# Twelve gate channel tiles done singly instead of ten, and operand roundings and sigmoids queued behind the weights in the output stage

## The chip, the cores and the metric

The kernel runs on one core of one Trainium2 chip. The metric is the device time of one execution in microseconds. The core's engines are TensorE (PE, with its weight loads shown apart as PEld), VectorE (DVE), ScalarE (ACT), GpSimd (POOL) and SyncE (SP). In this kernel SP and POOL issue the transfers. Every engine works through its own list of instructions in order and waits at an instruction until what it needs is there.

## The reference

One layer of a bidirectional encoder for two sequences, a prompt (b = 0) and a sample (b = 1), each 1024 rows by 1024 channels in float32. Cut to what matters here:

```
xn = rmsnorm(x, g_pre)
fv, fg, hv, hg, mg = split(xn @ w_in)
y_f = (real(fft2(fv)) * silu(fg)) @ w_fourier_out
v, x1, x2 = split(short_conv(hv, w_short))
z = v
for n, gate in enumerate((x1, x2)):
    z = gate * long_conv(z, filter_n)
y_h = (z * silu(hg)) @ w_hyena_out
g_f, g_h = split(sigmoid(mg + b_merge))
out = (g_f * y_f + g_h * y_h) @ w_out
y = x + rmsnorm(out, g_post)
```

The gates of a sequence are four sections of `xn @ w_in`, called by number in the kernel: 0 is `fg`, 4 is `hg`, 5 and 6 are the two halves of `mg`. Each has 1024 channels, which is 8 channel tiles of 128.

## The kernel before

**Numbers in two parts.** Float32 products are made on PE from operands split into a rounded part h and a remainder l: `split` (line 168) rounds with a copy on ACT and subtracts on DVE or POOL. A product is three matmuls, h·h, h·l and l·h (`mm3`, line 369; `times`, line 954). So before a weight or an operand can be used, it is loaded, rounded on ACT (tile `wh`, `sf`, `sh`) and subtracted (tile `wl` and the second part of `sf`, `sh`).

**Who sets the order.** The program is written as a sequence, and a scheduler gives each engine its list: it takes what its own model holds to be ready, and of that what stands earlier in the program. `with tc.issue_after(x)` puts everything in the block that runs on the engine of x behind x in that engine's list. It is an order of issue and no wait for the end of x, and it says nothing to other engines.

**The stages.** After the Fourier branch and the filters come, in this order:

1. The long convolutions (`branches`, line 897): for each sequence a list of 16 steps (sequence, order, channel tile). Step i traces the front of step i+1, then `conv_back` of step i (line 789; forward matmuls into `pX`, products with the filter on DVE, back matmuls into `pT`). For the second sequence the last steps also do gate channel tiles singly with `spill_gate` (line 757): `inproj` (line 714) multiplies all 8 blocks of the sequence by two weight halves into two PSUM tiles `pin`, ACT copies them out, SP stores them. Which tiles are done singly stands in `PLAIN` (line 969). Its tiles are taken from the end of the list: with four, three and two steps left, two each. The four that remain follow behind the last matmul of the last convolution (line 949).
2. The gates of the second sequence that are not in `PLAIN` (`phase_gates`, line 971): a pair of channel tiles (c, c+1) by two column halves is one job, done with seven products in place of eight, from sums of weights and sums of the sequence's blocks (`prepare` and `sums`). With the ten tiles in `PLAIN` there are 11 jobs. The tiles in PSUM are called `pg`.
3. The output stage (`phase_out`, line 1079): four units (sequence, half of the rows). A unit makes 8 projections by `w_fo` from the operands `sf` (tile `pyf`), then 8 by `w_ho` from the operands `sh` (`pyh`). `project` (line 1114) takes two weight halves, each loaded by POOL's queue in `weight` (line 1101), with three buffers in turn; each half is 12 matmuls. `operand` (line 1091) loads one of the 8 operand tiles of the next group and splits it at once, one in each projection. `gated` (line 1123) loads a gate tile by SP's queue, takes its sigmoid on ACT with a bias and multiplies the projection by it on DVE; gate tiles have three buffers. `beside` (line 1136) loads, rounds and sums blocks of `w_out` for the next stage, on ACT behind the sigmoid of its projection. In the last unit `sum4` loads and splits parts of a sum of `w_out` blocks (`t4`).
4. The last rows (`last_rows`), the product with `w_out` by seven products, tiles `po`.

Of the kernel before, what the change touches and what calls it, by code (L numbers as in the profile page):

```python
# [9 lines left out]
F32 = mybir.dt.float32  # L10
F32R = mybir.dt.float32r
I32 = mybir.dt.int32
AF = mybir.ActivationFunctionType
# [148 lines left out]
class K:  # L162
# [626 lines left out]
    def conv_back(self, n, ct, B, ws):  # L789
# [3 lines left out]
        for g, pairs in GROUPS:  # L793
# [34 lines left out]
            def tt(name):  # L828
                return ws.tile([P, 512], F32, tag="tt", name=name, bufs=4)
# [3 lines left out]
            elif g == 3:  # L833
                S_, D_ = tt("S"), T[1]
                self.add("dve", S_, T[1], Tp)
# [61 lines left out]
    def branches(self, nb, nct, ws):  # L897

        tc, nc = self.tc, self.nc
        steps = []
        for b in range(nb):
            steps.append((b, 0, 0))
            for c in range(1, nct):
                steps += [(b, 0, c), (b, 1, c - 1)]
            steps.append((b, 1, nct - 1))
        plain = list(self.PLAIN)
        Z, X = {}, {}

        def front(i):
            b, n, c = steps[i]
            src = self.conv(1, c, ws, "v", b) if n == 0 else Z.pop(c)
            return self.conv_front(src, ws)

        def gates(i):
            b, n, c = steps[i]
            x = self.conv(2 + n, c, ws, f"x{n + 1}", b)
            if n and b == 0:
                early = c < NH  # L920
                ps = None if early else self.inproj(4, c)
                for q in range(2):
                    sg = self.wp.tile([P, 512], F32, tag="gt", name="sg", bufs=3)
                    if early:
                        nc.sync.dma_start(sg, self.d_g[0][4][c][:, 512 * q:512 * q + 512])
                    nc.scalar.activation(sg, sg if early else ps[q], AF.Silu)
                    self.mul("pool", x[:, 512 * q:512 * q + 512], x[:, 512 * q:512 * q + 512], sg)
            X[i] = x
        B = front(0)
        gates(0)  # L930
        for i, (b, n, c) in enumerate(steps):
            nxt = None
            if i + 1 < len(steps):
                nxt = front(i + 1)
                gates(i + 1)
                if i + 2 < len(steps) and steps[i + 2][0] != steps[i + 1][0]:
                    self.load_x(steps[i + 2][0])
            y = self.conv_back(n, c, B, ws)
            B = nxt
            for _ in range({4: 2, 3: 2, 2: 2}.get(len(steps) - i, 0)):  # L940
                self.spill_gate(b, *plain.pop(), ws)
            z = self.gate(n, c, y, X.pop(i))
            if n == 0:
                Z[c] = z
                continue
            nc.sync.dma_start(self.d_sh[b][c], z)
            if b == 0 and NF <= c:
                self.spill_gate(0, 0, c, ws)
        with tc.issue_after(self.ended.ins):
            for sec, c in plain:  # L950
                self.spill_gate(1, sec, c, ws)
# [14 lines left out]
        self.stt("dve", s[:, 1], s[:, 0], -1.0, r[:, 3], MUL, SUB)  # L966
        self.add("dve", s[:, 3], s[:, 1], r[:, 2])

    PLAIN = [(5, 0), (5, 1), (6, 0), (6, 1), (5, 2), (5, 3), (6, 2), (6, 3), (5, 4), (5, 5)]

    def phase_gates(self):

# [3 lines left out]
        wp, b = self.wp, 1  # L976
        jobs = [(s, c) for c in range(0, 8, 2) for s in (0, 4, 5, 6) if (s, c) not in self.PLAIN]
        with ExitStack() as es:
# [100 lines left out]
    def phase_out(self):  # L1079
# [3 lines left out]
        tc, nc, a = self.tc, self.nc, self.a  # L1083
        wp, xp = self.wp, self.xp
        units = [(b, half) for b in range(NB) for half in range(2)]
        with ExitStack() as es:
# [4 lines left out]
            def operand(i, nm, k):  # L1091

                b, half = units[i]
                src = (self.d_g[b][0] if nm == "f" else self.d_g[b][4] if b else self.d_sh[b])[k][:, 512 * half:512 * half + 512]
                t = xp.tile([P, 2, 512], F32R, tag=f"x{'hl'[k // 4]}{k % 4 + 4 * (nm == 'h')}", name=f"s{nm}{k}", bufs=1)
                r = t[:, 1].bitcast(F32)
                nc.sync.dma_start(r, src)
                self.split(t[:, 0], t[:, 1], r, "dve", "act")
                return t[:, 0], t[:, 1]

            def weight(w, dt, q):


                own = self.nw % 3 == 2
                self.nw += 1
                pool, nb = (op, 1) if own else (wp, 2)
                r = pool.tile([P, 512], F32, tag="w", name="wr", bufs=nb)
                nc.gpsimd.dma_start(r, a[w][dt][:, 512 * q:512 * q + 512])
                h = pool.tile([P, 4, P], F32R, tag="wh", name="wh", bufs=nb)
                l = pool.tile([P, 4, P], F32R, tag="wl", name="wl", bufs=nb)  # L1110
                self.split(h.rearrange("p a b -> p (a b)"), l.rearrange("p a b -> p (a b)"), r, "dve", "act")
                return h, l

            def project(i, nm, w, dt, S):
                ps = self.psum("mm", 4, f"py{nm}")
                for q in range(2):
                    h, l = weight(w, dt, q)
                    for kk in range(4):
                        k = 4 * q + kk
                        self.mm3(ps, (h[:, kk], l[:, kk]), S[k], k == 0, k == 7)  # L1120
                return ps

            def gated(i, dt, ps, sec, bias, out):
                b, half = units[i]
                g = wp.tile([P, 512], F32, tag="gt", name="g", bufs=3)
                self.fetched = nc.sync.dma_start(g, self.d_g[b][sec][dt][:, 512 * half:512 * half + 512])
                self.opened = nc.scalar.activation(g, g, AF.Sigmoid, bias=self.bm[:, bias:bias + 1])
                out = g if out is None else out
                self.mul("dve", out, ps, g)
                return out  # L1130
# [51 lines left out]
            def sum4(k):  # L1182
                h, l = [sp.tile([P, 512], F32R, tag=f"yf{2 * k + j}", name=f"t4{'hl'[j]}{k}", bufs=1) for j in range(2)]
                r = l.bitcast(F32)
                nc.sync.dma_start(r, self.d_t[1][:, k])
                self.split(h, l, r, "dve", "act")
                T4.append((h, l))

            with tc.issue_after(self.copied.ins):
                S = {(0, "f"): [operand(0, "f", k) for k in range(8)]}  # L1190
            gp = oc.tile([P, D], F32, name="gp")
            nc.sync.dma_start(gp, a["g_post"][0].partition_broadcast(P))
            for i, (b, half) in enumerate(units):
                Yf = []
                S[i, "h"] = []
                for dt in range(8):
                    ps = project(i, "f", "w_fo", dt, S[i, "f"])
                    S[i, "h"].append(operand(i, "h", dt))
                    y = sp.tile([P, 512], F32, tag=f"yf{dt}", name=f"yf{dt}", bufs=1)
                    Yf.append(gated(i, dt, ps, 5, dt, y))  # L1200
                    beside(i, dt)
                S[i + 1, "f"] = []
                for dt in range(8):
                    ps = project(i, "h", "w_ho", dt, S[i, "h"])
                    if i + 1 < len(units):
                        S[i + 1, "f"].append(operand(i + 1, "f", dt))
                    g = gated(i, dt, ps, 6, 8 + dt, None)
                    self.add("dve", Yf[dt], Yf[dt], g)
                    nc.sync.dma_start(self.d_m[i][:, :, dt], Yf[dt].rearrange("p (t c) -> p t c", t=4))
                    beside(i, 8 + dt)  # L1210
                    if i == 3 and dt % 2 == 1:
                        sum4(dt // 2)
            block = lambda j: [(BH[k][:, j], BL[k][:, j]) for k in range(4)]
            T = [[(TH[k][:, j], TL[k][:, j]) for k in range(4)] for j in range(2)]
            self.last_rows(units, block(0), block(1), block(2), T1, T[0], T[1], T4, gp, op)
# [196 lines left out]
```

## Time and profile before

| | |
|---|---|
| median of 3 runs | 2494.66 us (2486.66 to 2496.76) |
| the profiled execution | 2485.07 us, span 2483.2 us, granted TensorE clock 0.997 |
| PE busy | 2407.4 us, 97% of the span, 13184 matmuls |
| PE weight load busy | 2081.4 us, 84% |
| DVE busy | 1955.9 us, 79% |
| ACT busy | 1102.2 us, 44% |
| POOL busy | 498.6 us, 20% |
| moved by DMA | 429.39 MB, mean 173 GB/s |

The span runs from the first to the last instruction of the profiled execution; 1.9 us of its time lie around it. A matmul is shown with a modelled length that reaches over the start of the next one, so the time that one really takes is the distance from its start to the next start. In rows of instructions in order of time the first number is the start in us from the start of the span, the second the length; "x4" joins four instructions that follow each other, and the bracket gives the idle time of the engine ahead of the row and what ended it. In rows of waits, "A <- B: 70.2, 49, 5.5" says that the instruction A waited for B for 70.2 us in 49 cases, 5.5 us at most.

### The profile page before, as it was taken

The page shows a single profiled execution, that of the slowest core. Times are in us where ns is not written, and L with a number is a line of the kernel's source. Part 1 is how long each engine was busy: PE and PEld are TensorE (multiplying, and loading weights), DVE is VectorE, ACT ScalarE, POOL GpSimd, SP SyncE. Part 2 cuts the span into 40 slices and gives each one's busy share as a digit, 9 for nine tenths or more (in the row PEclk, how much of TensorE's full clock was granted, in tenths as well). Part 3 has the DMA queues.
Part 4 walks back from the last instruction along what each step waited for, and adds up shares of the span by engine and source line. Part 5 has one row for each costly group of instructions (what it writes and reads, how often), then busy time and mean ns, then how long its engine had stood idle before and what let it go on. Part 6 is the DMA issues. An engine that isn't in the chain of part 4 may idle for free.

```text
span 2483.2 us, 37239 instructions
## 1 busy us (share of the span) xinstructions
PE 2407.4 (97%) x13184; PEld 2081.4 (84%) x13184; DVE 1955.9 (79%) x3737; ACT 1102.2 (44%) x2043; POOL 498.6 (20%) x514
## 2 busy tenths in 40 slices
PE   6999999999989999999999999999999999999998
PEld 6988888888878888888888888887888787878786
DVE  7786788888798999999889999876655456655677
ACT  5546666666653333333222233333443445444443
POOL 1331222212233333441000000212000111212121
PEclk9999999999999999999999999999999999999999
DMA  7536545444555554545343443435443567675543
GB/s 272 191 113 225 196 157 162 162 163 158 177 184 184 180 174 167 171 154 193 123 149 137 137 141 123 140 132 182 168 163 136 196 219 252 237 245 201 161 166 127
DMA packets 224867, 429.39 MB, mean 173 GB/s; under 512 B 23510, under 2 KB 87223, under 8 KB 224168
## 3 DMA queue, kind: packets, MB, share of 16 engines
q1 hardware_dynamic: 197868, 332.29, 40.1%
q0 software_dynamic: 26624, 94.70, 10.9%
q8 instruction: 104, 1.70, 0.3%
q14 instruction: 83, 0.68, 0.1%
q10 hardware_dynamic: 188, 0.02, 0.0%
HBM read 290.60 MB, written 136.31 MB: 172 GB/s over the span
## 4 chain that ended last, share of the span: by engine, by line
PE 44%; DMA 5%; DVE 3%; issue 1%; ACT 1%; SPq 0%; DVEq 0%; POOL 0%; ACTq 0%
PE pin L194 14%; PE pg L194 8%; PE po L194 6%; PE pyf L194 5%; PE pT L194 4%; PE pyh L194 4%; PE pX L194 3%; DMA oraw<-in_w_out 1%; PE tph L785 1%; DMA xraw<-d_x 1%; DMA mraw<-d_m 1%; DMA sh<-d_g 1%; DMA wr<-in_w_fo 1%; DMA wh<-d_w 0%; DMA d_m<-yf 0%
## 5 line engine op out<-in xcount | busy, mean ns | idle before, releaser
L194 PE MATMUL pin<-xh,wh 128*128 128x512 f32 x1440 | 563.8, 392 | 4.4 <-DVE v L177 1.8
L194 PE MATMUL pin<-xh,wl 128*128 128x512 f32 x1440 | 563.0, 392 | 1.6 <-POOL wl L181 1.6
L194 PE MATMUL pin<-xl,wh 128*128 128x512 f32 x1440 | 564.2, 392 | 0.0
L181 POOL TENSOR_TENSOR wl<-wr,wh 128x512 fp32r<-128x512 f32 x132 | 250.0, 1895 | 1132.2 <-ACT wh L171 1093.5
L194 PEld LDWEIGHTS pin<-xh,wh 128*128 128x128 f32 x1440 | 271.1, 188 | 54.6 <-DVE v L177 2.0
L194 PEld LDWEIGHTS pin<-xh,wl 128*128 128x128 f32 x1440 | 271.3, 188 | 51.6 <-POOL wl L181 2.5
L194 PEld LDWEIGHTS pin<-xl,wh 128*128 128x128 f32 x1440 | 271.3, 188 | 49.5
L171 ACT CAST wh<-wr 128x512 fp32r<-128x512 f32 x260 | 159.8, 618 | 227.2 <-PE pin L194 102.6
L194 PE MATMUL pT<-cinv,yh 128*128 128x256 f32 x1024 | 193.2, 283 | 0.5 <-ACT yh L171 0.5
L194 PEld LDWEIGHTS pT<-cinv,yh 128*128 128x128 f32 x1024 | 165.5, 191 | 10.1 <-ACT yh L171 0.9
L181 DVE TENSOR_TENSOR t<-pX,k 128x1024 f32<-128x1024 f32 x128 | 155.6, 1216 | 11.0 <-PE pX L194 7.6
L194 PE MATMUL pyh<-sh,wh 128*128 128x512 f32 x512 | 157.9, 391 | 3.5 <-ACT wh L171 3.5
L194 PE MATMUL pX<-bh,cfwd 128*128 128x256 f32 x768 | 160.4, 287 | 0.6 <-DVE t L181 0.6
L194 PE MATMUL pyf<-sf,wh 128*128 128x512 f32 x512 | 157.6, 391 | 1.6 <-ACT wh L171 1.6
L194 PE MATMUL pT<-cinv,yl 128*128 128x256 f32 x512 | 145.8, 285 | 5.1 <-DVE yl L181 5.0
L171 ACT CAST yh<-y 128x512 fp32r<-128x512 f32 x128 | 79.7, 622 | 158.6 <-DVE y L181 125.5
L171 ACT CAST bh<-b 128x512 fp32r<-128x512 f32 x144 | 88.9, 621 | 119.5 <-DVE b L181 81.2
L181 DVE TENSOR_TENSOR wl<-wr,wh 128x512 fp32r<-128x512 f32 x128 | 87.2, 686 | 67.1 <-ACT wh L171 67.0
L194 PEld LDWEIGHTS pX<-bh,cfwd 128*128 128x128 f32 x768 | 125.5, 190 | 4.0 <-DVE t L181 1.0
L181 DVE TENSOR_TENSOR bl<-b,bh 128x512 fp32r<-128x512 f32 x144 | 110.3, 767 | 21.9 <-ACT bh L171 21.8
L194 PEld LDWEIGHTS pyh<-sh,wh 128*128 128x128 f32 x512 | 95.5, 188 | 25.4 <-ACT wh L171 6.2
L194 PEld LDWEIGHTS pyf<-sf,wh 128*128 128x128 f32 x512 | 95.6, 188 | 23.1 <-ACT wh L171 3.7
(348 smaller groups left out, 5385.6 us busy)
## 6 DMA issues: line engine op xcount, KB each, us to landing
k<-d_k SPq DMA_DIRECT2D x128, 512.0 KB, 4.0
wr<-in_w_in SPq DMA_DIRECT2D x132, 256.0 KB, 3.1
d_g<-gt SPq DMA_DIRECT2D x124, 256.0 KB, 2.3
d_k<-kt SPq DMA_DIRECT2D x128, 128.0 KB, 2.2
d_k<-kt SPq DMA_DIRECT2D x64, 256.0 KB, 2.3
wr<-in_w_fo POOLq DMA_DIRECT2D x64, 256.0 KB, 3.6
g<-d_g SPq DMA_DIRECT2D x64, 256.0 KB, 3.9
wr<-in_w_ho POOLq DMA_DIRECT2D x64, 256.0 KB, 3.5
```

Of the source, the lines that this page charges most:

```text
L171: self.rounded = nc.scalar.copy(h, src)
L181: e.tensor_tensor(out, a, b, op=op)
L194: return self.nc.tensor.matmul(out, lhsT, rhs, start=start, stop=stop, skip_group_check=shared)
L785: nc.tensor.transpose(tp[:, q * P:(q + 1) * P], eo[:, e, q], self.ident)
```

## The change

There are two parts. In the first, tiles (6, 4) and (6, 5) join `PLAIN`, so they are done singly, their job leaves the seven-product stage (10 jobs stay), and the last step takes two tiles as the three before it do. The pairs move by one step, since they are taken from the end of the list.

In the second, the loading and the splitting of an operand in the output stage are two functions. `weight` keeps the instruction with which ACT rounds the latest weight half (`self.weighed`). The new function `ahead` splits the operand that the projection before has loaded, on ACT behind that rounding, and loads the next one; after the last projection of a group it is called once more for the last split. The sigmoid of a gate, too, is queued on ACT behind the rounding of the second weight half of its projection. The first eight operands of the first unit are split at once as before.

```diff
@@ branches
-            for _ in range({4: 2, 3: 2, 2: 2}.get(len(steps) - i, 0)):
+            for _ in range({4: 2, 3: 2, 2: 2, 1: 2}.get(len(steps) - i, 0)):
                 self.spill_gate(b, *plain.pop(), ws)
-    PLAIN = [(5, 0), (5, 1), (6, 0), (6, 1), (5, 2), (5, 3), (6, 2), (6, 3), (5, 4), (5, 5)]
+    PLAIN = [(5, 0), (5, 1), (6, 0), (6, 1), (5, 2), (5, 3), (6, 2), (6, 3), (5, 4), (5, 5), (6, 4), (6, 5)]
@@ phase_out
-                r = t[:, 1].bitcast(F32)
-                nc.sync.dma_start(r, src)
-                self.split(t[:, 0], t[:, 1], r, "dve", "act")
+                nc.sync.dma_start(t[:, 1].bitcast(F32), src)
+                return t
+
+            def rounded(t):
+                self.split(t[:, 0], t[:, 1], t[:, 1].bitcast(F32), "dve", "act")
                 return t[:, 0], t[:, 1]
...
                 self.split(h.rearrange("p a b -> p (a b)"), l.rearrange("p a b -> p (a b)"), r, "dve", "act")
+                self.weighed = self.rounded
                 return h, l
...
+            def ahead(i, nm, dt):
+
+                S_ = S.setdefault((i, nm), [])
+                with tc.issue_after(self.weighed.ins):
+                    if dt:
+                        S_[-1] = rounded(S_[-1])
+                if dt < 8:
+                    S_.append(operand(i, nm, dt))
+
             def gated(i, dt, ps, sec, bias, out):
...
-                self.opened = nc.scalar.activation(g, g, AF.Sigmoid, bias=self.bm[:, bias:bias + 1])
+                with tc.issue_after(self.weighed.ins):
+                    self.opened = nc.scalar.activation(g, g, AF.Sigmoid, bias=self.bm[:, bias:bias + 1])
...
-                S = {(0, "f"): [operand(0, "f", k) for k in range(8)]}
+                S = {(0, "f"): [rounded(operand(0, "f", k)) for k in range(8)]}
...
                 for dt in range(8):
                     ps = project(i, "f", "w_fo", dt, S[i, "f"])
-                    S[i, "h"].append(operand(i, "h", dt))
+                    ahead(i, "h", dt)
...
-                S[i + 1, "f"] = []
+                ahead(i, "h", 8)
                 for dt in range(8):
                     ps = project(i, "h", "w_ho", dt, S[i, "h"])
                     if i + 1 < len(units):
-                        S[i + 1, "f"].append(operand(i + 1, "f", dt))
+                        ahead(i + 1, "f", dt)
...
+                if i + 1 < len(units):
+                    ahead(i + 1, "f", 8)
```

More of the change, by code (lines that the diff above doesn't have):

```diff
@@ L1194, in phase_out @@
                 Yf = []
-                S[i, "h"] = []
                 for dt in range(8):
                     ps = project(i, "f", "w_fo", dt, S[i, "f"])
-                    S[i, "h"].append(operand(i, "h", dt))
+                    ahead(i, "h", dt)
                     y = sp.tile([P, 512], F32, tag=f"yf{dt}", name=f"yf{dt}", bufs=1)
```

## The prediction

> **What bounds the kernel now.** I read first the busy time of each engine by stretch, with the borders laid where the TensorE (PE) output tile changes its name: the last convolution, the four gate tiles after it, the seven-product gate stage, the output projections with their gates (the output stage), the last rows, and at the end the step before the last convolution. The columns are the stretch, its length, then busy time and instruction count of PE, PE weight load, DVE, ACT and POOL, the granted clock, the share of the DMA engines and GB/s.
>
> ```profile
> 1681.71:1701.42 19.71, 14.60 (x95) 12.96 (x94) 13.51 (x18) 5.29 (x9) 2.02 (x2) 0.91 0.33 108
> 1701.42:1744.51 43.09, 43.09 (x191) 35.66 (x190) 28.32 (x31) 16.93 (x22) 11.83 (x10) 1.00 0.64 224
> 1744.51:1955.50 210.99, 210.04 (x925) 173.15 (x924) 120.64 (x172) 85.45 (x140) 11.60 (x22) 1.00 0.45 156
> 1955.50:2319.80 364.30, 355.25 (x1538) 286.12 (x1538) 206.65 (x315) 167.91 (x270) 68.16 (x127) 1.00 0.68 227
> 2319.80:2483.20 163.40, 152.73 (x673) 125.81 (x671) 122.65 (x254) 64.84 (x134) 31.95 (x29) 0.98 0.44 148
> 1640.00:1681.71 41.71, 41.71 (x232) 36.42 (x232) 30.97 (x57) 12.37 (x21) 8.15 (x5) 1.00 0.31 102
> ```
>
> PE is the bound in nearly all of them, and the busy column hides by how much, because the modelled length of a matmul overlaps the next one. The pitch is the measure. In the second stretch 190 matmuls of 128x512 start (191 are touched): 43.09 / 190 = 0.227 us each. By the code a channel tile done singly is 2 weight halves x 2 column halves x 4 blocks x 3 passes = 48 matmuls, 10.9 us; a pair by seven products is 7 x 4 x 3 = 84, 19.1 us. At that pitch the gate stage (11 pairs, 924 matmuls) needs 209.7 us and takes 210.99: it is full. The output stage (4 units x 16 projections x 24 = 1536) needs 348.4 us and takes 364.30: it loses **15.9 us**. The last convolution I price from the order of PE instructions in time (start, length, what):
>
> ```profile
> 1681.71 1.05 PE L194 MATMUL pX<-b,cfw 128*128 128x128 f32 x8
> 1682.52 0.36 PE L194 MATMUL pX<-bh,cfwd 128*128 128x256 f32 x1
> ...
> 1688.30 0.28 PE L194 MATMUL pT<-cinv,yl 128*128 128x256 f32 x1
> 1688.42 0.40 PE L194 MATMUL pT<-cinv,yh 128*128 128x256 f32 x2
> ```
>
> Eight small matmuls take 0.81 us (1681.71 to 1682.52), and one of 256 columns has a pitch of 0.12 us (1688.30 to 1688.42). The convolution has 3 groups x 12 forward and 4 x 12 back, 84 x 0.12 = 10.1 us; with the 0.8 and the first two matmuls of the gate tile behind it (0.45) that is 11.3 us of work in 19.71: **8.4 us lost**, 5.1 of it as PE idle (19.71 - 14.60), the rest as small gaps and a clock that fell to 0.91 on the mean. So PE loses 8.4 + 15.9 = 24.3 us in the two places that the change touches.
>
> Why the output stage loses them shows in the waits there, first of ACT (total us, times, longest), then in rows of PE (in brackets the idle time and its releaser) and of ACT:
>
> ```profile
> ACT g L1127 <- DMA g<-d_g: 70.2, 49, 5.5
> ...
> ACT sh L171 <- DMA sh<-d_g: 14.0, 11, 3.9
> ACT sf L171 <- DMA sf<-d_g: 13.2, 11, 3.0
> ACT sh L171 <- DMA sh<-d_sh: 10.7, 9, 3.5
> ACT t4h L171 <- DMA t4l<-d_t: 8.2, 3, 3.7
> ```
>
> ```profile
> 1969.46 0.73 PE L194 MATMUL pyf<-sf,wh 128*128 128x512 f32 x2 [1.20 <-ACT wh L171]
> ...
> 2193.33 0.50 PE L194 MATMUL pyh<-sh,wl 128*128 128x512 f32 x1 [1.09 <-DVE wl L181]
> ...
> 2202.79 1.26 PE L194 MATMUL pyh<-sh,wh 128*128 128x512 f32 x4 [1.45 <-ACT wh L171]
> 2204.92 0.50 PE L194 MATMUL pyh<-sh,wl 128*128 128x512 f32 x1 [0.87 <-DVE wl L181]
> ...
> 2299.32 0.73 PE L194 MATMUL pyh<-sh,wh 128*128 128x512 f32 x2 [0.77 <-ACT wh L171]
> ```
>
> ```profile
> 2187.81 1.97 ACT L171 CAST sf<-sf 128x512 fp32r<-128x512 f32 x3 [2.24 <-DMA sf<-d_g]
> 2189.68 0.61 ACT L171 CAST wh<-wr 128x512 fp32r<-128x512 f32 x1
> ...
> 2199.09 0.73 ACT L1127 ACTIVATE g<-g,bm 128x512 f32<-128x512 f32 x1 [4.86 <-DMA g<-d_g]
> 2199.72 1.56 ACT L171 CAST bh<-oraw 128x512 fp32r<-128x512 f32 x2
> 2201.18 1.04 ACT L171 CAST th<-osum 128x1024 fp32r<-128x1024 f32 x1
> 2202.12 1.14 ACT L171 CAST wh<-wr 128x512 fp32r<-128x512 f32 x2
> ...
> 2298.13 0.62 ACT L171 CAST t4h<-t4l 128x512 fp32r<-128x512 f32 x1 [2.24 <-DMA t4l<-d_t]
> ```
>
> PE never waits for an operand or a gate itself. It waits for a rounded weight (wh from ACT, then wl from DVE) that stood in ACT's order behind something that waited for a transfer: at 2187.81 three operand roundings (sf) after 2.24 us for their DMA, at 2199.09 a sigmoid after 4.86 us and then 2.6 us of w_out roundings, at 2298.13 a rounding of t4. The five PE rows fall into operands 1.20 + 1.09 = 2.29, sigmoid with w_out 1.45 + 0.87 = 2.32, t4 0.77, together 5.38. I split the 15.9 us in these shares: 6.8, 6.9 and 2.3.
>
> **The change part by part.** *Two tiles more done singly, one pair less by seven products.* PE: +96 - 84 = +12 matmuls x 0.227 = **+2.7 us**. With the pair go its DVE sums, its roundings and its two weight loads; DVE is busy 120.64 of 210.99 us there, so that saves nothing. The tile list is taken from its end, so each earlier step now takes the pair after its old one, of equal shape; only the last step gets work it did not have.
>
> *That work beside the last convolution.* 96 matmuls, 21.8 us, come to a place with 8.4 us lost. The convolution is traced first and the two tiles fill what it leaves. Bounds: all 8.4 us come back, or none, if the tiles stand wholly before it. Nearest in kind is the last row of the first fence, the step just before (1640 to 1681.71), in which two gate tiles already stand beside a convolution and PE is busy for all of 41.71 us; so I take 7.7 and leave 0.7 for the first wait. On SP's queue the two tiles bring four weight loads and four stores of 0.25 MB, 2 MB over some 33 us or 60 GB/s more where the DMA engines are 0.33 used at 108 GB/s. A stall of the convolution's chain is late for nobody then: its result is only stored for a job of the gate stage, and the four tiles behind its last matmul still give the preparation of that stage the same 43 us. Sum of this part: +2.7 - 7.7 = **-5.0 us** (between -5.7 and +2.7).
>
> *Roundings of operands behind weights.* The loads stay in the same iteration, so SP is given the same transfers in the same program order; 32 + 24 roundings move one projection later and, on ACT, behind the second weight half of the projection just traced. A landed operand costs ACT one cast there, 0.6 us, and no wait. Cover: three weight buffers let a rounding run ahead until PE is done with the weight three before, so two weights of 12 x 0.227 = 2.7 us each, 5.4 us, stand between ACT and PE; without it each rounding would cost PE its 0.6 us. The 6.8 us go, but for half of the share of the first stall (1.20 / 2.29 x 6.8 / 2 = 1.8), since at the start the weights' own loads also wait for the gate stage to free their buffers: **-5.0 us**.
>
> *Sigmoid behind weights.* The waits of 70.2 us are for gate loads. Behind the second weight half of its own projection, the sigmoid is asked for when PE is still a projection and a half (36 matmuls, 8.2 us) from needing it, and a load that took 5.5 us longest to wait for has mostly landed. The w_out roundings are queued behind the sigmoid (line 1138) and move with it, so at 2202.12 the held-up weight goes in front of them. What stays is their own 2.6 us on ACT and the subtractions on DVE; I leave 40% of 6.9 and take **-4.1 us**. t4's 2.3 us stay. If the order only moves the stalls to other weights, both gains are nothing; if all goes, 15.9 are won: bounds -15.9 and, with every stall doubled, +15.9.
>
> Sum: -5.0 - 5.0 - 4.1 = **-14.1 us**. The profiled execution took 2485.07 us (span 2483.2), so 2471.0 of its kind; it lay 9.6 below the median of the runs, 2494.66. I subtract from the median: **2480.6**, said as 2481.
>
> [...]
>
> **The rivals.** *B, the output stage keeps its stalls.* For it: the rounding of a weight waits for PE's release too, and POOL issues each weight load only after DVE's subtraction. Against: the stalls above all have a transfer wait in front of them. Price: only -5.0, time 2490. *C, the two tiles run before the convolution and not beside it.* For it: their inputs are ready earlier than the convolution's. Against: the step before it alternates. Price: +2.7 - 9.1 = -6.4, time 2488. *D, slower: the sigmoid gets late.* Place: the multiplication by the gate on DVE, behind which the next weights' subtractions stand. Today 70.2 us of gate loads are waited for where they cost less than 15.9; if a load lands over 8.2 us after the weight rounding in front of its sigmoid, the multiplication is late and holds up wl in each of the 49 cases; at the rate that these waits cost now the loss doubles, +15.9 - 5.0 = +10.9, time 2506, and more where the delay goes on to the next bank. *E, nearly all stalls go:* +2.7 - 8.4 - 15.9 = -21.6, time 2473.
>
> **How the numbers follow.** Forecast 0.54 (own range 2475 to 2487), B 0.16, C 0.12, D 0.10, E 0.08. The bound for no change is 0.5%, 12.5 us, about what a measurement of this kernel can tell from nothing. The forecast's -14.1 lies just beyond it: about two thirds of its chance, 0.36, with E's 0.08 and 0.02 of C's upper tail is faster, 0.46. Slower by over 0.5% is most of D, whose delay can go on as said, 0.08. The rest, 0.46, is within. The range leaves out half of D above and the deepest part of E with a run like the profiled one below: 2466 to 2499.
>
> **What would show it.** The stretch of the last convolution with its two tiles should have no PE idle over 1 us and a clock of 1.00; the gate stage should be shorter by 19.1 us. ACT's wait of g for d_g should fall from 70.2 to under 20 us, and those of sf and sh for DMA from 37.9 to under 5. PE's loss in the output stage should be near 7 us, the t4 stalls unchanged. Wrong if the gate stage starts with new waits, if the idle time beside the last convolution stays, or if DVE's multiplications wait for ACT g.

## The result and the profile after

The changed kernel takes 2481.0 us (median of 11 runs, 2472.59 to 2486.31); the kernel before, run beside it, takes 2491.92 us (11 runs, 2484.89 to 2498.11). The ratio is 0.9957, with a 95% interval from 0.9945 to 0.9970: 10.9 us less. The profiled execution of the changed kernel took 2480.27 us, with a span of 2478.1 us.

The busy time by stretch, with the borders at the same changes of PE's output tile as before (the last convolution with its two added tiles, the four gate tiles behind it, the gate stage, the output stage, the last rows):

```profile
1684.10:1705.90 21.80, 21.80 (x138) 19.74 (x137) 13.13 (x16) 6.85 (x12) 4.12 (x3) 1.00 0.38 121
1705.90:1760.70 54.80, 54.07 (x238) 44.43 (x238) 34.55 (x37) 21.02 (x27) 17.70 (x15) 1.00 0.67 230
1760.70:1951.10 190.40, 190.40 (x841) 157.72 (x840) 105.65 (x153) 76.62 (x128) 9.99 (x19) 1.00 0.46 155
1951.10:2310.30 359.20, 353.70 (x1537) 288.39 (x1536) 205.65 (x314) 163.22 (x270) 67.60 (x126) 1.00 0.70 230
2310.30:2478.10 167.80, 154.37 (x673) 127.05 (x671) 122.80 (x254) 64.98 (x134) 31.44 (x29) 0.97 0.46 145
```

Beside the last convolution PE is busy for all of 21.80 us, at a clock of 1.00 (before 14.60 of 19.71 us, at 0.91). Part of the added work stands behind the convolution, so the second row grew; the two rows together went from 62.80 to 76.60 us, 13.80 more for 21.8 us of added matmuls. The gate stage shrank from 210.99 to 190.40 us, one job less, and is full: 840 x 0.2268 = 190.5. The output stage shrank by 5.1 us. But the last rows grew from 163.40 to 167.80 us, and there the change edits nothing.

The waits of ACT in the output stage (total us, times, longest):

```profile
ACT wh L171 <- PE pyf L194: 63.0, 38, 7.2
...
ACT g L1140 <- DMA g<-d_g: 27.3, 11, 4.8
...
ACT t4h L171 <- DMA t4l<-d_t: 14.6, 3, 6.1
```

The sigmoid waits 27.3 us for its gate (before 70.2), and no row with sf or sh waiting for a transfer is left (before 37.9 us in three rows). ACT now mostly waits for PE to release a weight, 118.7 us in 75 cases with pyf and pyh together, while PE itself waits for 5.1 us in the whole stage; ACT's waits for the weights' own loads grew from 10.2 us (7 cases) to 30.9 us (17 cases). PE in the same stage, the rows with an idle time over 1 us:

```profile
1964.79 0.73 PE L194 MATMUL pyf<-sf,wh 128*128 128x512 f32 x2 [1.92 <-ACT wh L171]
...
2111.82 0.50 PE L194 MATMUL pyh<-sh,wl 128*128 128x512 f32 x1 [1.65 <-DVE wl L181]
...
2289.77 0.73 PE L194 MATMUL pyh<-sh,wh 128*128 128x512 f32 x2 [1.16 <-ACT wh L171]
```

and what stood on ACT in front of these weights:

```profile
1963.51 0.72 ACT L1140 ACTIVATE g<-g,bm 128x512 f32<-128x512 f32 x1 [3.06 <-DMA g<-d_g]
1964.13 0.60 ACT L171 CAST wh<-wr 128x512 fp32r<-128x512 f32 x1
...
2105.73 0.73 ACT L1140 ACTIVATE g<-g,bm 128x512 f32<-128x512 f32 x1 [2.30 <-DMA g<-d_g]
2106.36 1.56 ACT L171 CAST bh<-oraw 128x512 fp32r<-128x512 f32 x2
2107.82 1.04 ACT L171 CAST th<-osum 128x1024 fp32r<-128x1024 f32 x1
2108.76 1.14 ACT L171 CAST wh<-wr 128x512 fp32r<-128x512 f32 x2
...
2288.58 0.62 ACT L171 CAST t4h<-t4l 128x512 fp32r<-128x512 f32 x1 [4.68 <-DMA t4l<-d_t]
```

Three stalls are left: at the start of the stage a sigmoid whose gate lands late holds a weight back; near 2106 it is the w_out roundings, which moved with the sigmoid and now hold the next pair of weights; and t4 as before.

The last rows, first before, then after, as rows in order of time (POOL issues the load of mraw, ACT rounds it and then copies u, PE waits for u):

```profile
2322.09 1.57 POOL L1229 DMA_DIRECT2D mraw<-d_m  x3 [16.67 <-DVE wl L181]
...
2329.20 1.67 ACT L171 CAST wh<-mraw 128x512 fp32r<-128x512 f32 x3 [5.93 <-DMA mraw<-d_m]
...
2331.39 0.56 ACT L1259 COPY u<-po 128x512 f32<-128x512 f32 x1
...
2332.01 0.50 PE L194 MATMUL po<-t1h,mxh 128*128 128x512 f32 x1 [1.22 <-ACT u L1259]
```

```profile
2312.81 1.58 POOL L1243 DMA_DIRECT2D mraw<-d_m  x3 [16.84 <-DVE wl L181]
...
2322.30 1.66 ACT L171 CAST wh<-mraw 128x512 fp32r<-128x512 f32 x3 [8.45 <-DMA mraw<-d_m]
...
2324.48 0.56 ACT L1273 COPY u<-po 128x512 f32<-128x512 f32 x1
...
2325.10 0.80 PE L194 MATMUL po<-t1h,mxh 128*128 128x512 f32 x1 [3.72 <-ACT u L1273]
2325.69 0.63 PE L194 MATMUL po<-t1l,mxh 128*128 128x512 f32 x1
2326.12 1.05 PE L194 MATMUL po<-t1h,mxh 128*128 128x512 f32 x2
...
2328.25 0.47 PE L194 MATMUL po<-t1l,mxh 128*128 128x512 f32 x1
2328.56 0.63 PE L194 MATMUL po<-t1h,mxh 128*128 128x512 f32 x2
```

u is needed by PE at once, but on ACT it stands behind three roundings for the next rows, and these wait for mraw. From the issue of mraw to its first rounding it is 7.1 us before and 9.5 us after, so PE waits 3.72 us instead of 1.22. After the wait a matmul takes 0.43 us (2325.69 to 2326.12) until 2328.25 and 0.23 us later: that is the second part of the loss, over 1 us more.

### The profile page after: what moved, and what is told of

The parts are those of the page before. It is cut to its first block, busy times and chain, and to the rows that moved or that the text cites. A ratio compares the mean times of both kernels' runs of the same rounds, so it can differ in the third digit from the quotient of the medians.

```text
span 2478.1 us, 37219 instructions
## 1 busy us (share of the span) xinstructions
PE 2411.1 (97%) x13196; PEld 2090.5 (84%) x13196; DVE 1947.7 (79%) x3725; ACT 1093.0 (44%) x2041; POOL 500.6 (20%) x516
## 4 chain that ended last, share of the span: by engine, by line
PE 49%; DMA 3%; DVE 1%; ACT 0%; issue 0%; POOL 0%; SPq 0%; DVEq 0%; ACTq 0%; POOLq 0%
PE pin L194 16%; PE pg L194 8%; PE pyf L194 7%; PE po L194 6%; PE pyh L194 4%; PE pT L194 4%; PE pX L194 4%; DMA mraw<-d_m 1%; PE tph L785 1%; DMA d_m<-yf 0%; DMA d_g<-gt 0%; DMA t4l<-d_t 0%; DMA g<-d_g 0%; DMA wh<-d_w 0%; DMA sf<-d_g 0%
## 5 line engine op out<-in xcount | busy, mean ns | idle before, releaser
L194 PE MATMUL pin<-xh,wh 128*128 128x512 f32 x1472 | 577.5, 393 | 3.7 <-DVE v L177 1.8
L194 PE MATMUL pin<-xl,wh 128*128 128x512 f32 x1472 | 578.0, 393 | 0.0
L194 PE MATMUL pin<-xh,wl 128*128 128x512 f32 x1472 | 576.6, 393 | 0.7 <-POOL wl L181 0.7
L194 PEld LDWEIGHTS pin<-xh,wh 128*128 128x128 f32 x1472 | 278.0, 189 | 54.5 <-DVE v L177 2.0
L194 PEld LDWEIGHTS pin<-xh,wl 128*128 128x128 f32 x1472 | 278.1, 189 | 51.9 <-POOL wl L181 1.5
L194 PEld LDWEIGHTS pin<-xl,wh 128*128 128x128 f32 x1472 | 278.0, 189 | 50.6
```

The costliest lines, as they stand in the source:

```text
L194: return self.nc.tensor.matmul(out, lhsT, rhs, start=start, stop=stop, skip_group_check=shared)
```

## The experiments

The theory after the result: part one and part two save about what was forecast, and the last rows give some of it back because u stands behind the wait for mraw. The rivals: the gain of a part is smaller than thought and the last rows differ by chance; or mraw's place in a queue moved. Each ratio below is to the kernel before, run in turns on the same chip.

**Each part alone.** The first kernel has the two added singles only, the second the output stage's new order only.

```diff
-            for _ in range({4: 2, 3: 2, 2: 2}.get(len(steps) - i, 0)):
+            for _ in range({4: 2, 3: 2, 2: 2, 1: 2}.get(len(steps) - i, 0)):
...
-    PLAIN = [..., (5, 4), (5, 5)]
+    PLAIN = [..., (5, 4), (5, 5), (6, 4), (6, 5)]
```

> Part one alone: twelve tiles done singly, output stage as before. Theory (the two parts add, and part one is a refill of idle PE time): 2.7 us more matmuls, the 8.4 us lost beside the last convolution come back and the start of the gate stage loses its 1 us, so 6 to 7 us less than before (ratio 0.9972 to 0.9976); the gate stage near 190 us, the output stage still near 364 us with its stalls, the first wait for ACT u in the last rows near 1.2 us. Rival (all of the gain belongs to the output stage): ratio 1.000.

Measured: 2489.74 us, ratio 0.9996 (0.9985 to 1.0007). A miss: the whole did not become faster by what can be measured. The gate stage did what it should, the last rows grew as in the whole change, with the same cause:

```profile
1764.80:1955.90 191.10, 190.63 (x842) 157.51 (x841) 105.50 (x153) 77.31 (x130) 9.46 (x18) 1.00 0.46 155
1955.90:2320.70 364.80, 353.88 (x1536) 286.56 (x1537) 206.59 (x315) 166.64 (x269) 68.13 (x127) 1.00 0.69 226
2320.70:2489.00 168.30, 155.31 (x673) 127.77 (x671) 122.81 (x254) 65.00 (x134) 31.44 (x29) 0.96 0.45 144
```

```profile
2335.12 0.80 PE L194 MATMUL po<-t1h,mxh 128*128 128x512 f32 x1 [3.38 <-ACT u L1259]
```

> Part two alone: ten tiles done singly. Theory: the output stage 4 to 6 us shorter than before (358 to 360 us), but the wait for ACT u in the last rows near 3.7 us instead of 1.2, so the whole 0 to 5 us less (ratio 0.998 to 1.000). Rival (the longer wait in the last rows is a matter of the single execution and not of the order): wait near 1.2 us, ratio 0.9975 to 0.9982.

Measured: 2485.35 us, ratio 0.9976 (0.9962 to 0.9990). PE waits 2.01 us for u and the last rows take 165.9 us. The ratio is the rival's, the wait for u lies between theory and rival. In the last rows the two singles alone cost 4.9 us and the new order alone 2.5 us against the kernel before, one reading each; so both parts may have a share in it, and which is larger isn't shown.

**The two halves of part two.** In the first kernel the sigmoid keeps its old place, in the second the operands' roundings do; both have the twelve singles.

```diff
-                with tc.issue_after(self.weighed.ins):
-                    self.opened = nc.scalar.activation(g, g, AF.Sigmoid, bias=self.bm[:, bias:bias + 1])
+                self.opened = nc.scalar.activation(g, g, AF.Sigmoid, bias=self.bm[:, bias:bias + 1])
```

> The change without the sigmoid's place: operands behind weights, sigmoid free. Theory (the sigmoid behind weights caused the longer stall at the start of the output stage, where a gate load is waited for 3.1 us in front of a weight, and cured part of the stalls by the w_out roundings): the stall at the start falls from 4.2 us to under 2, those by the w_out roundings are again near 5 us, the whole equal to the change within 2 us. Rival (the sigmoid's place does the work, the operands' does not): 3 us or more slower than the change.

Measured: 2484.86 us, ratio 0.9972 (0.9959 to 0.9984). By the ratios that is 3.7 us slower than the change, as the rival has it, though the intervals overlap. What the theory blamed on the sigmoid's new place is there in its old place too: at the start of the stage the sigmoid waits 2.95 us for its gate and PE 1.81 us behind it.

```diff
-                with tc.issue_after(self.weighed.ins):
-                    if dt:
-                        S_[-1] = rounded(S_[-1])
                 if dt < 8:
-                    S_.append(operand(i, nm, dt))
+                    S_.append(rounded(operand(i, nm, dt)))
```

> The change without the operands' place: sigmoid behind weights, operands split at once as before. Theory: stalls by operands after the start are back (3.6 us), the stall at the start stays near 4 us, so 3 to 4 us slower than the change. Rival (the operands' place does nothing): equal to the change within 1 us.

Measured: 2481.50 us, ratio 0.9962 (0.9947 to 0.9978). The output stage takes 361.8 us with the operands' move alone and 361.4 us with the sigmoid's alone, against 364.8 us with neither (the singles alone) and 359.2 us with both. PE's waits in the stage add up to 6.4, 7.5, 10.9 and 5.1 us in the same order. By these readings either move removes part of the stalls and the two gains don't simply add, but kernels with both moves differ among themselves by as much (355.0 to 361.7 us), so how the gain is shared between the moves isn't shown. On the whole the operands' move adds nothing to the sigmoid's that can be measured (0.9962 to 0.9957).

**u in front of the roundings.** The preparation of the next rows is queued behind the copy of u, nothing else is changed.

```diff
+            first_out = self.kept_at
...
-                A = prepare(i + 1)
+                with tc.issue_after(first_out.ins):
+                    A = prepare(i + 1)
```

On the whole change:

> The change, and in the last rows the roundings of the next pair's rows are queued on ACT behind the copy u. Theory (part of the gain of the change is given back because u stands on ACT behind roundings that wait 8 us for mraw, PE waits 3.7 us for u and its clock falls after it): last rows 167.8 us fall to 162.5 to 164, no wait for u over 0.5 us, the whole 4 to 5 us less than the change (near 2476.5, ratio to before near 0.9938). Rival (PE would wait for the same rows a little later anyway): a wait of 2 us or more for wh or wl of mraw in its place, 0 to 1.5 us less.

Measured: 2477.22 us, ratio 0.9944 (0.9930 to 0.9958), last rows 163.1 us. The last rows fell as the theory has it; on the whole the interval overlaps that of the change (0.9945 to 0.9970). On the two singles alone:

> Part one alone, with u in front of the roundings in the last rows. Theory (part one wins 6 us between the last convolution and the output stage and lost 4.9 of them again in the last rows): 5 us less than part one alone and 6 to 7 less than before (ratio 0.9972 to 0.9977). Rival (part one wins nothing on the whole for another reason): ratio 0.999 or more.

Measured: 2488.24 us, ratio 0.9989 (0.9979 to 0.9998), last rows 163.2 us. That is a miss: the whole is much nearer to the rival (0.999 or more) than to the theory. PE no longer waits for u in either. ACT in the first of the two:

```profile
2316.03 0.59 ACT L1273 COPY u<-po 128x512 f32<-128x512 f32 x1 [1.25 <-PE po L194]
...
2317.86 1.14 ACT L171 CAST wh<-mraw 128x512 fp32r<-128x512 f32 x2 [1.24 <-DMA mraw<-d_m]
```

The copy now waits for PE and not for a transfer, and the last rows are as long as in the kernel before. But in these two kernels mraw was also there sooner, 7.8 and 7.5 us after its issue against 9.5 us in the change, so it isn't shown that u's place alone took off the 4.7 and 5.1 us by which the last rows shrank.

**Why mraw lands later.** One job's weight loads are issued twice, so that POOL's queue carries as many transfers as with ten singles.

```diff
                 for i in range(2):
-                    nc.gpsimd.dma_start(r[:, 2 * i:2 * i + 2].rearrange("p a b -> p (a b)"), a["w_in"][sec, c + i])
+                    for _ in range(1 + ((sec, c) == jobs[4])):
+                        nc.gpsimd.dma_start(r[:, 2 * i:2 * i + 2].rearrange("p a b -> p (a b)"), a["w_in"][sec, c + i])
```

> The change, with the two weight loads of one seven-product job issued twice, so that POOL's queue carries as many loads before the last rows as before the change; the second pair of loads only writes the same bytes again. Theory under test (mraw lands 9.3 to 9.8 us after its issue with twelve singles and 7.4 to 7.9 us with ten, because two loads fewer move where POOL's queue stands): landing back under 8 us, the wait for u 1.2 to 2 us, last rows 163 to 166 us. Rival (the place in the queue has nothing to do with it): landing over 9 us, last rows 167 us or more.

Measured: 2482.79 us, ratio 0.9959 (0.9940 to 0.9977); mraw 8.0 us after its issue, PE's wait for u 2.33 us, last rows 166.7 us. It lies between both expectations and settles nothing.

**The price of the parts with u in front.** Three kernels on one chip: the kernel before with u in front, the output stage's new order with u in front, and the whole change with u in front a second time.

> The kernel before (ten singles, no change in the output stage's order) with one edit: in the last rows' row-group loop the next group's roundings stand behind the first output block's copy u. In the kernel before PE waits only 1.22 us for u. Theory (the copy behind the mraw roundings costs the twelve-singles kernels 3 to 4 us more than the ten-singles kernels): last rows 162 to 163.5 us (163.4 before), whole 0 to 1.5 us less, ratio 0.9993 to 1.0000. Rival (the copy's place is worth the same 4 us in every kernel, the difference of last rows lies elsewhere): last rows near 159, ratio near 0.998.

Measured: 2490.34 us, ratio 1.0006 (0.9994 to 1.0018), last rows 162.2 us. With ten singles u's place is worth nothing that can be measured, so its worth is not a general one; the rival falls.

> The output stage's part of the change alone (ten singles) with u first. Compared with the run of the whole change with u first, this prices the two more singles when their give-back in the last rows is taken away. Theory (part one saves 5 us and the last rows gave 3 of them back): convolutions and gates together near 1212 against 1207, last rows near 163 in both, whole 4 to 5.5 us over the change with u first, ratio near 0.9963. Rival (part one is worth nothing even so): within 1.5 us of the change with u first.

Measured: 2481.80 us, ratio 0.9971 (0.9959 to 0.9984).

> The whole change with u first, a second time, beside the run with ten singles on the same chip: ratio 0.993 to 0.996 as before, convolutions and gates near 1207, output stage near 355 to 359, last rows near 163.

Measured: 2479.21 us, ratio 0.9955 (0.9941 to 0.9969). Ratio and first stages are as expected (1206.5 us), the output stage (360.7 us) and the last rows (166.2 us) are longer than expected, and the ratio is that of the change itself (0.9957): a gain on the whole from u's place is not shown. The two singles are worth 2.6 us here by the medians of this chip and 4.0 us by the ratios, between theory and rival. Why the last rows are long again shows in this run:

```profile
2315.21 1.58 POOL L1243 DMA_DIRECT2D mraw<-d_m  x3 [16.81 <-DVE wl L181]
...
2321.03 0.59 ACT L1273 COPY u<-po 128x512 f32<-128x512 f32 x1 [1.26 <-PE po L194]
...
2324.36 1.14 ACT L171 CAST wh<-mraw 128x512 fp32r<-128x512 f32 x2 [2.74 <-DMA mraw<-d_m]
...
2328.94 0.50 PE L194 MATMUL po<-bh,wl 128*128 128x512 f32 x1 [2.11 <-DVE wl L181]
```

u is in time, but mraw is there only 9.2 us after its issue (2324.36 - 2315.21), and now PE waits for the subtraction behind its rounding. So u's place is only the first thing that a late mraw meets. From the issue to the first rounding it is 7.0 to 7.6 us in the four kernels with ten singles (mean 7.3) and 7.5 to 9.5 us in the eight with twelve in which that rounding waits for the transfer (mean 8.6); the ranges touch. What makes it later stays open.

**A version that beats both.** First, with u in front, the roundings of t4 are queued behind a weight, or behind u, instead of where their load is:

```diff
+            def split4(k):
+                h, l = T4[k]
+                with tc.issue_after(self.weighed.ins):
+                    self.split(h, l, l.bitcast(F32), "dve", "act")
...
                         sum4(dt // 2)
+                        if dt >= 5:
+                            split4((dt - 5) // 2)
...
+            if i == 0:
+                with tc.issue_after(first_out.ins):
+                    for h, l in T4[2:]:
+                        self.split(h, l, l.bitcast(F32), "dve", "act")
```

> As the change with u first, and the roundings of the parts of t4 two projections of the group later, the last two behind u. Theory: the 2.6 us lost in the output stage behind t4 go as well, output stage near 356.5 us, the whole 6 to 7 us less than the change (near 2474.5). Rival (t4 then arrives late in the last rows): a wait of PE for t4h or t4l in the last rows, no gain beside that of u.

Measured: 2475.34 us, ratio 0.9932 (0.9916 to 0.9949); the t4 stalls are gone and the last rows take 162.2 us. Then the w_out roundings of a block are also spread over three projections:

```diff
-                        elif part == 3:
-                            blocks(k, self.raw)
+                        elif part in (3, 4, 5):
+                            blocks(k, self.raw, part - 3)
```

> The whole change, u first, the last transposed operand's roundings deferred, and the output matrix's blocks split over the steps of three input projections instead of one. Theory (ACT's queue of four roundings in one piece makes PE wait near 2110 us; spread they fit between the weights' roundings): no PE wait over 1 us there, output stage 352 to 354 us, whole 1 to 3 us under the version without the split, ratio 0.991 to 0.9925. Rival (the pieces only make three small waits of one large one): output stage 355 or more, ratio 0.993 or above.

Measured: 2470.79 us, ratio 0.9922 (0.9908 to 0.9937): 19.9 us under the kernel before on its chip. The intervals of the last two overlap, so the step between them is not shown by the time alone, but PE's waits in the output stage show it; these are all:

```profile
PE pyf L194 <- ACT wh L171: 3.1, 1, 3.1
PE pyf L194 <- DVE wl L181: 0.4, 1, 0.4
```

and on ACT one rounding of a block stands in front of a weight instead of three, the first being `bh`:

```profile
2108.87 0.73 ACT L1140 ACTIVATE g<-g,bm 128x512 f32<-128x512 f32 x1 [1.74 <-DMA g<-d_g]
2109.50 0.60 ACT L171 CAST bh<-oraw 128x512 fp32r<-128x512 f32 x1
2110.01 0.62 ACT L171 CAST wh<-wr 128x512 fp32r<-128x512 f32 x1
```

Only the stall at the start is left. That keeps the stage at 354.7 us, 0.7 over what was expected.

## Why the prediction was right, and where it was not

The same code has not the same length in two profiled executions: up to the first matmul of the long convolutions nothing is changed in any of these kernels, and that took from 743.2 to 750.6 us; the output stage of one kernel profiled twice took 355.0 and 360.7 us. A term of a few us can't be read from one pair of profiles. So I take means over all kernels that share the code of a stage, with the range of their readings (in the gate stage that takes in the kernel with two loads issued twice).

| | predicted | with the old code | with the new code | difference |
|---|---|---|---|---|
| long convolutions and gate stage | -5.0 | 1212.3 (4 readings, 1211.8 to 1213.0) | 1206.8 (10, 1204.8 to 1209.5) | -5.5 |
| output stage | -9.1 | 366.8 (4, 364.3 to 369.6) | 359.0 (6, 355.0 to 361.7) | -7.9 |
| last rows, u behind the roundings; ten singles, then twelve | 0 | 164.7 (2, 163.4 and 165.9) | 167.7 (5, 166.7 to 168.5) | +3.0 |
| sum | -14.1 | | | -10.4 |

The sum lies near the measured 10.9 us, but not closer than its terms are known: the 165.9 us are those of the new order alone, and with the kernel before by itself (163.4) the last rows are +4.3 and the sum is -9.1.

**The total.** 2481 was forecast and 2481.0 measured, but that is luck: two errors cancel in it. The forecast took 14.1 us off the median of three runs, 2494.66; eleven runs of the kernel before have 2491.92, 2.7 us lower. And the change saved 3.2 us less than forecast (10.9 against 14.1).

**Work beside the last convolution, -5.0.** Right in its stages, with its mechanism: -5.5 as a mean, with ranges that don't overlap, and -6.8 in the two profiles shown (+13.80 - 20.59). Beside the last convolution PE has no idle time and the clock stays at 1.00; of the 96 added matmuls 43 stand in the first row after the change and 47 in the second, so C, in which the tiles run ahead of the convolution, is out. One DVE instruction beside the convolution got longer, without harm to PE: an addition that ran while POOL subtracted an added tile's weight took 1.32 us, where the one of the same form before it took 0.69 us:

```profile
1697.59 1.29 POOL L181 TENSOR_TENSOR wl<-wr,wh 128x512 fp32r<-128x512 f32 x1 [11.80 <-ACT wh L171]
```

```profile
1693.56 0.69 DVE L181 TENSOR_TENSOR y<-t 128x512 f32<-128x512 f32 x1
...
1698.12 1.32 DVE L181 TENSOR_TENSOR y<-t 128x512 f32<-128x512 f32 x1
```

PE had the added matmuls to do in that time.

By the ratios of whole times the two singles are worth less in each comparison: 1.0 us alone and 4.7 us on top of the new order (0.9976 to 0.9957), 2.7 and 4.0 us with u in front. The last rows are a place where the rest can go; that they take all of it isn't shown.

**The step that failed: nothing was booked for the last rows.** The forecast costed what the change does to stages that it edits and looked no further. The row that would have warned stood in the profile before: PE waited 1.22 us for u, which stood behind roundings with a wait of 5.93 us in front. With twelve singles and u behind the roundings PE waited 2.33 to 3.72 us for u in five kernels, with ten singles 1.22 and 2.01 us in two, and the last rows grew by 3.0 us as a mean. With u in front they go from 167.7 to 163.1, 163.2 and 166.2 us; part of that may be mraw, which landed sooner in the first two.

**Operands behind weights, -5.0, and sigmoid behind weights, -4.1.** Their sum of -9.1 measured -7.9. The waits fell as forecast for sf and sh (none left) and not quite for the sigmoid (27.3 us against under 20). PE's own waits in the stage bear the mechanism out: 8.5 to 12.0 us in the four kernels with the old code (mean 10.2), 3.3 to 7.8 us in the six with the new (mean 5.6). But the loss that stays is larger than forecast: 359.0 - 348.4 = 10.6 us as a mean after the change and not near 7, since the old code's mean lay 2.5 us above the profile that the forecast was worked out from, and the gain was 1.2 us smaller.

The shares were wrong. They were taken from five of PE's twelve waits (5.38 of 8.5 us), and one of the five was booked in the wrong place: the 1.20 us at 1969.46 went to the operands, but what stood on ACT in front of that weight was a sigmoid:

```profile
1968.17 0.72 ACT L1127 ACTIVATE g<-g,bm 128x512 f32<-128x512 f32 x1 [1.35 <-DMA g<-d_g]
1968.80 0.60 ACT L171 CAST wh<-wr 128x512 fp32r<-128x512 f32 x1
```

With all twelve waits sorted by what stands in front of them on ACT, the sigmoid with w_out has 5.0 us, the operands 2.5 and t4 1.0. The half that the operands' term kept for the first stall therefore had the wrong cause as well. That stall didn't shrink (1.20 us was PE's longest wait there before, 1.92 us after): it ends when the second gate has landed, and the sigmoid that takes it starts 12.65 us after the stage's first matmul before and 12.40 us after the change (12.09 us with the sigmoid in its old place, 10.5 to 13.4 us in all the kernels). Neither edit brings that load forward. The w_out roundings were left 40% of 6.9 = 2.8 us. The stall of 2.32 us near 2203 that stood for them is gone; another near 2111, three waits with 1.48 us in all before, is still there with 1.65 us. t4 stayed, with waits of 1.16 and 0.39 us (0.77 and 0.25 before).

**The other rivals.** B, in which the output stage keeps its stalls, is out by 7.9 us. D, the late sigmoid, shows in two places, at the start and near 2106, where it holds a weight. At the start it holds DVE's multiplication too, one of the forecast's signs of being wrong, but as in the kernel before: 4.4 us in two cases, against 2.6 us in two cases then.

```profile
1964.26 0.69 DVE L181 TENSOR_TENSOR yf<-pyf,g 128x512 f32<-128x512 f32 x1 [3.09 <-ACT g L1140]
```

So D's mechanism shows there, and not at the many gates that its price needs. E, in which nearly all stalls go, needed three more edits: u in front, t4's roundings later and the w_out roundings spread; that version is 20 us under the kernel before.

## What to carry to other kernels

When one wait is taken away on an engine, look at what stands behind the next wait in its list, also in stages that the change doesn't touch: here a copy that PE needs at once stood on ACT behind roundings for later, which waited 5.93 us for a transfer before and 8.45 us after, and a transfer that landed 2.4 us later became 2.5 us more of a wait of PE. Queue work that waits for a transfer behind work that feeds the bounding engine, and in small pieces. Where two stalls hold the same instruction, price the two edits together.

## What the hardware showed beside that

Some waits of PE cost more here than their length, and some did not. After the 1.92 us at the start of the changed kernel's output stage the matmuls first go on at their usual pace and then slow down, as PE's rows in order of time show, with the row of the stretch behind them (granted clock 0.50):

```profile
1966.66 1.05 PE L194 MATMUL pyf<-sf,wh 128*128 128x512 f32 x2
1967.51 0.63 PE L194 MATMUL pyf<-sf,wl 128*128 128x512 f32 x1
1967.94 1.06 PE L194 MATMUL pyf<-sf,wh 128*128 128x512 f32 x2
...
1970.05 0.39 PE L194 MATMUL pyf<-sf,wl 128*128 128x512 f32 x1
1970.28 0.62 PE L194 MATMUL pyf<-sf,wh 128*128 128x512 f32 x2
```

```profile
1966.70:1970.00 3.30, 3.30 (x9) 2.60 (x8) 0.14 (x1) 0.80 (x2) 0.54 (x1) 0.50 0.58 178
```

From 1966.66 to 1970.05, 3.4 us, a matmul takes 0.43 us (1967.51 to 1967.94), then 0.23 us again: 8 matmuls, 1.6 us lost, nearly as much as the wait. The wait of 1.65 us at 2111.82 had no such end. In the part of the 14 profiles behind 1900 us, PE has 42 waits of 1 us or more. Of the 14 from 1.92 us up, 13 were followed by a granted clock of 0.50 (the one of 2.49 us in the two singles with u in front was not); of the 28 up to 1.86 us, 5 were. The matmuls were slow for 3.4 us here and for 3.2 us after the wait of 3.72 us for u; after the wait of 3.38 us in the singles alone it was 5.3 us. What decides whether the clock falls, and for how long, isn't shown.
